# A two-layer hybrid decoder on one core: level sums and pooling from GpSimd to VectorE, the sample state's output product turned round

## The chip, the cores and the metric

The kernel runs on one core of one Trainium2 chip. The metric is the device time of one execution in microseconds (us), as a median of several runs; less is better.

## What is computed

Two layers of a decoder are run for 256 prompt tokens and 8 sample sequences of 8 tokens each, 320 tokens together (T = 320), with shared weights in float32. Cut to what matters here:

```python
def mixer(h, s_gla, buf, pos0, ...):
    proj = h @ w_in                       # q, k, v, g, a low-rank gate input, u
    gk = log_sigmoid(gk_lr @ w_gk_up + b_gk) / 16
    o, s_new = gla(q, k, v, gk, s_gla)    # S_t = diag(a_t) S_{t-1} + k_t^T v_t ; o_t = q_t S_t, a_t = exp(gk_t)
    o = rmsnorm(o, gla_norm) * silu(g)
    p, buf_new = pool_mixer(u, buf, ...)  # group i: trailing mean over (2, 4, 8, 16)[i] positions, minus the token
    return concatenate([o, p]) @ w_out, s_new, buf_new

def trunk(x, ...):
    for l in range(2):
        x = x + mixer(rmsnorm(x, norm_mix[l]), ...)
        h = rmsnorm(x, norm_ffn[l])
        x = x + (silu(h @ w_gate[l]) * (h @ w_up[l])) @ w_down[l]
    return rmsnorm(x, norm_final), states, buffers
```

There are 4 heads with keys of 128 and values of 256, a width of 2048 and a feed-forward width of 5632. The samples start from a state S of 128 x 256 for each sequence and head; the prompt starts from zero.

## The kernel before

Activations stand transposed: 128 channels on the partitions, the 320 tokens along the row, 16 such tiles for the width (`xT`). A weight is streamed in units of 128 x 1024 float32 (four tiles in the contraction, two in the output). Each unit is loaded by SP's queue (`raw`, four buffers), split by ScalarE into a rounded part and by VectorE into the rest (`hl`, three buffers, L115 and L116), and multiplied in three matmuls per tile (L151 to L153): rounded weight with rounded activation, rounded weight with the activation's rest, the weight's rest with the rounded activation. One unit is 24 matmuls, a unit of the pooling's weights 12.

`run` walks through the list of units. Before the matmuls of a unit it issues loads up to five units ahead and splits up to two units ahead; after them it gives each of the generators in `self.gens` one step. What a generator emits in its step so stands on its engine's queue behind the splits of that unit. Every engine works its queue in order. Small matmuls are put into a queue of their own by `add_small`, and `beside` places them one by one between the triples of the units' matmuls; `placed` lets a generator wait until they all stand.

What the change touches, in the order of the program:

- `first_squares`: the sum of squares of the input over the 16 tiles, for the first normalisation, and the masks' conversion. It runs beside the first units, while the input tiles (`xT`) are split into `xh` and `xl` (L118, L119).
- `level_gen`: the decays of the prompt and the samples, in eight doublings of a block length s. `P` holds the running sums of the log gates from a block's start, `X` those to a block's end, both in the tile `PX`. Each doubling takes exponentials on ScalarE (L446, L452, L456), multiplies them with q and k on VectorE (L458 to L463), adds to X on GpSimd (L466) and to P on VectorE (L468), and multiplies blocks on TensorE (L428). At s = 4 the samples' sums are complete: `e8` is their exponential, `q8` that times q.
- `ev_u` and `pool_gen`: four groups, i = 3, 2, 1, 0 with windows 16, 8, 4, 2. `ev_u` evicts the product into `EP` (prompt) and `ES` (samples) on VectorE (L595, L596) and copies the old buffer, loaded into `stg` by SP, in front of it on GpSimd (L598). `pool_gen` doubles the window on GpSimd (L614 into `AP`, L615 into `AS`), corrects the first positions (L621), copies the new buffer into `so` (L625, L626), and forms the difference `d` on VectorE, which is split into `dh` and `dl` for a pooling unit.
- `head_gen`: for each head the transposes of v, the output product, its squares and its norm, and the new states. `S` holds four sequences' states, two buffers of 128 x 4 x 256 for a head. The samples' part of the output takes, for each of 8 sequences and 2 halves of the values, one matmul with S as the weight and 8 columns of `q8` moving (L743).
- `finish`: the last norm. `rsqrt` takes a logarithm and an exponential on ScalarE and four steps on VectorE; then VectorE and GpSimd multiply the 16 tiles (L1017) and SP stores them (L1018).

The line of the old output product, and the part of `stack`, `EP` and `so` that the steps below name, are these:

```python
            for b in range(NB):
                self.add_small(224, lambda b=b: nc.tensor.matmul(
                    po[:, NP + 8 * b : NP + 8 * b + 8], S[b // 4][:, b % 4, vc],
                    st["q8"][:, h, 8 * b : 8 * b + 8], start=False, stop=(b == NB - 1)))
```

Of the kernel before, what the change touches and what calls it, by code (L numbers as in the profile page):

```python
# [66 lines left out]
class Decoder:  # L67
    def __init__(self, tc, ctx, a):
        self.tc, self.nc, self.a = tc, tc.nc, a
        nc = self.nc  # L70
        pool = lambda name, bufs, **k: ctx.enter_context(tc.tile_pool(name=name, bufs=bufs, **k))
        self.const = const = pool("const", 1)
        self.act = pool("act", 1)
        self.ffb = pool("ffb", 2)
        self.wp = pool("wp", 1)
        self.nrm = pool("nrm", 1)
        self.keep = pool("keep", 1)
        self.acc = pool("acc", 4, space=PSUM)
# [241 lines left out]
    def open_early(self):  # L320
# [7 lines left out]
        st["q8"] = self.keep.tile([P, H, 64], F32, tag="q8", name="q8")  # L328
        st["e8"] = self.keep.tile([P, H, 64], F32, tag="e8", name="e8")
# [73 lines left out]
    def level_gen(self):  # L403
# [35 lines left out]
        for li, s in enumerate((1, 2, 4, 8, 16, 32, 64, 128)):  # L439
# [26 lines left out]
            nc.gpsimd.tensor_tensor(Xv[:, :, :, 0, :], Xv[:, :, :, 0, :],  # L466
# [118 lines left out]
    def ev_u(self, ps, i):  # L585
# [12 lines left out]
        nc.gpsimd.tensor_copy(ES[:, :, :, 0:BUF], stg)  # L598
        self.gens.append(self.pool_gen(l, i, EP, ES))

    def pool_gen(self, l, i, EP, ES):
# [8 lines left out]
        while s < w:  # L610
# [3 lines left out]
            nc.gpsimd.tensor_tensor(ap[:, :, lo:], cp[:, :, lo:], cp[:, :, lo - s : np_ - s], ALU.add)  # L614
            nc.gpsimd.tensor_tensor(as_[:, :, lo:], cs[:, :, lo:], cs[:, :, lo - s : ns_ - s], ALU.add)  # L615
# [5 lines left out]
        nc.gpsimd.tensor_tensor(cp[:, :, BUF : BUF + 16], cp[:, :, BUF : BUF + 16],  # L621
# [3 lines left out]
        nc.gpsimd.tensor_copy(so[:, :, 0:NB, :], ES[:, :, :, NS:])  # L625
        nc.gpsimd.tensor_copy(so[:, :, NB, :], EP[:, :, NP:])  # L626
# [39 lines left out]

    def head_gen(self, h, vT):
# [10 lines left out]
        S = []  # L678
        for qd in range(2):
            s = late.tile([P, 4, DV], F32, tag="S", name="S", bufs=2)  # L680
            nc.sync.dma_start(out=s, in_=a["s0"][l, h, :, 4 * qd : 4 * qd + 4])
            S.append(s)
# [28 lines left out]
        o = late.tile([P, 2, T], F32, tag="o", name="o", bufs=2)  # L711
        sq = late.tile([P, 2, T], F32, tag="osq", name="osq")
# [12 lines left out]
        def state_out(qd, pss):  # L725
            for b4 in range(4):
                b = 4 * qd + b4
                nc.vector.scalar_tensor_tensor(
                    S[qd][:, b4, :], S[qd][:, b4, :], st["e8"][:, h, 8 * b + 7 : 8 * b + 8],
                    pss[b4 // 2][:, 256 * (b4 % 2) : 256 * (b4 % 2) + 256], ALU.mult, ALU.add)  # L730
            nc.sync.dma_start(out=a["s_sample"][l, h, :, 4 * qd : 4 * qd + 4], in_=S[qd])

        def out_mm(c):
# [5 lines left out]
                po[:, 128:NP], vt[:, 1, vc], self.sc[:, h, 256:384], start=False, stop=True))  # L739
            self.add_small(220, lambda: nc.tensor.matmul(  # L740
                po[:, NP:T], vs[:, vc], self.scs[:, h, :], start=True, stop=False))
            for b in range(NB):
                self.add_small(224, lambda b=b: nc.tensor.matmul(  # L743
                    po[:, NP + 8 * b : NP + 8 * b + 8], S[b // 4][:, b % 4, vc],
                    st["q8"][:, h, 8 * b : 8 * b + 8], start=False, stop=(b == NB - 1)))
            return po

        def out(c, po):
            nc.scalar.activation(o[:, c, :], po[:, :T], AF.Copy, scale=self.vec(l, V_GN, c))
            nc.scalar.activation(sq[:, c, :], po[:, :T], AF.Square)  # L750

        pos = [out_mm(0), out_mm(1)]
        yield
        yield from self.placed()
        pss = state_mm(0)
        for c in range(2):
            out(c, pos[c])
# [10 lines left out]
        pss = state_mm(1)  # L768
        yield
        yield from self.placed()  # L770
        sp = late.tile([P, 2, T], F32, tag="osq", name="sp")[:, 0, :DV]
        nc.scalar.copy(sp, pS[:, :DV])
        nc.sync.dma_start(out=a["s_prompt"][l, h], in_=sp)
        state_out(1, pss)
        ro = late.tile([P, T], F32, tag="ro", name="ro")
# [181 lines left out]
    def first_squares(self):  # L957
        nc = self.nc
        q = [self.ffb.tile([P, 8, T], F32, tag=t, name="q" + t) for t in ("ah", "al")]
        for c in range(2):  # L960
            x = self.xT[:, 4 * c : 4 * c + 4, :]
            nc.gpsimd.tensor_tensor(q[0][:, 4 * c : 4 * c + 4, :], x, x, ALU.mult)
        add = lambda a, b: nc.gpsimd.tensor_tensor(a, a, b, ALU.add)
        add(q[0][:, 0:4], q[0][:, 4:8])
        for c in range(2):
            for _ in range(2):
                yield
            v = q[1][:, 4 * c : 4 * c + 4]
            nc.scalar.activation(v, self.xT[:, 8 + 4 * c : 12 + 4 * c, :], AF.Square)
            if c == 0:  # L970
                add(q[0][:, 0:4], v)
                v = q[0]
            add(v[:, 0:2], v[:, 2:4])
            add(v[:, 0], v[:, 1])
# [27 lines left out]
    def finish(self, evacs):  # L1002
# [4 lines left out]
        nc.scalar.activation(self.warm, self.eps, AF.Ln)  # L1007
# [106 lines left out]
```

## Time and profile before

| what | value |
|---|---|
| runs | 2706.63, 2707.62, 2709.3 us; median 2707.62 |
| the profiled execution | 2707.78 us, of which the span from the first to the last instruction 2706.0 us |
| TensorE busy | 2670.5 us (99% of the span) |
| VectorE busy | 1353.6 us (50%) |
| ScalarE busy | 1067.7 us (39%) |
| GpSimd busy | 310.6 us (11%) |
| DMA | 409.06 MB, mean 151 GB/s |

The execution lies 0.16 us above the median of the runs. PE is TensorE, PEld its weight loads, DVE VectorE, ACT ScalarE, POOL GpSimd, SP the engine on whose queue all DMAs are issued. In a timeline a row has the start, the duration (of all instructions of the row, where there are several), the engine, the line, the operation, what it writes and reads, its shape and its count; in brackets the engine's idle time before it and what ended that. A matmul's own duration overlaps that of the next: what one costs is read from the distance of the starts.

### The profile page before, as it was taken

What the parts mean: (1) busy time and instruction counts of PE and PEld (TensorE: products, weight loads), DVE (VectorE), ACT (ScalarE), POOL (GpSimd) and SP (SyncE); (2) the same over time, 40 slices, a digit from 0 to 9 for tenths busy, and PEclk for the clock granted to TensorE, in tenths of its full rate; (3) what the DMA queues carried; (4) which work ended last, traced back from release to release, by engine and by line L of the source; (5) the groups of instructions that cost most, each with busy time, mean ns of one, the idle gap of its engine ahead of it and who ended that gap; (6) DMA issues with size and microseconds to landing.
All of it is one profiled execution on the core that took longest, in us unless ns stands there. A gap on an engine that the chain in (4) does not pass through costs nothing.

```text
span 2706.0 us, 44907 instructions
## 1 busy us (share of the span) xinstructions
PE 2670.5 (99%) x19046; PEld 2649.3 (98%) x19046; DVE 1353.6 (50%) x1662; ACT 1067.7 (39%) x1346; POOL 310.6 (11%) x347
## 2 busy tenths in 40 slices
PE   9999999999999999999999999999999999999997
PEld 8999999999999999999999999999999999999997
DVE  7754554544444444444658545445444444444444
ACT  5445544333333333333444554443333333333334
POOL 3521211000000000000106111100000000000002
PEclk9999999999999999999999999999999999999999
DMA  5455544444444444444443555544444444444443
GB/s 195 124 157 175 170 153 149 148 149 152 151 148 149 151 152 150 148 150 151 146 152 107 170 179 164 152 148 149 148 150 151 151 148 149 150 152 150 148 150 108
DMA packets 116217, 409.06 MB, mean 151 GB/s; under 512 B 13360, under 2 KB 16944, under 8 KB 116016
## 3 DMA queue, kind: packets, MB, share of 16 engines
q1 hardware_dynamic: 116016, 406.19, 47.9%
q8 instruction: 149, 2.44, 0.4%
q14 instruction: 52, 0.43, 0.0%
HBM read 392.98 MB, written 13.16 MB: 150 GB/s over the span
## 4 chain that ended last, share of the span: by engine, by line
PE 93%; issue 2%; DVE 2%; POOL 1%; ACT 1%; DMA 0%; DVEq 0%; SPq 0%; ACTq 0%; POOLq 0%
PE acc L151 31%; PE acc L153 30%; PE acc L152 30%; PE ps_o L743 1%; DVE hl L116 1%; POOL PX L466 0%; ACT hl L115 0%; POOL AS L615 0%; POOL AP L614 0%; PE ps_sn L719 0%; PE ps_o L736 0%; PE ps_sp L766 0%; PE ps_o L740 0%; DMA raw<-in_w_in 0%; DVE xT L1017 0%
## 5 line engine op out<-in xcount | busy, mean ns | idle before, releaser
L116 DVE TENSOR_TENSOR hl<-raw,hl 128x1024 fp32r<-128x1024 f32 (+1 forms) x729 | 923.3, 1267 | 1250.6 <-ACT hl L115 1249.6
L115 ACT CAST hl<-raw 128x1024 fp32r<-128x1024 f32 (+1 forms) x729 | 759.8, 1043 | 1291.1 <-PE acc L153 1244.4
L151 PE MATMUL acc<-xh,hl 128*128 128x320 f32 x3840 | 1212.0, 316 | 1.7 <-ACT xh L118 0.9
L153 PE MATMUL acc<-xh,hl 128*128 128x320 f32 x3840 | 1188.0, 309 | 4.2 <-DVE hl L116 4.2
L152 PE MATMUL acc<-xl,hl 128*128 128x320 f32 x3840 | 1187.4, 309 | 1.4 <-DVE xl L119 1.3
L151 PEld LDWEIGHTS acc<-xh,hl 128*128 128x128 f32 x3840 | 722.0, 188 | 6.8 <-issue 1.7
L153 PEld LDWEIGHTS acc<-xh,hl 128*128 128x128 f32 x3840 | 721.5, 188 | 5.9 <-DVE hl L116 5.6
L152 PEld LDWEIGHTS acc<-xl,hl 128*128 128x128 f32 x3840 | 722.4, 188 | 4.3 <-DVE xl L119 2.0
L153 PE MATMUL acc<-ah,hl 128*128 128x320 f32 x1408 | 435.1, 309 | 0.0
L151 PE MATMUL acc<-ah,hl 128*128 128x320 f32 x1408 | 435.1, 309 | 0.0
L152 PE MATMUL acc<-al,hl 128*128 128x320 f32 x1408 | 435.1, 309 | 0.0
L151 PEld LDWEIGHTS acc<-ah,hl 128*128 128x128 f32 x1408 | 264.3, 188 | 0.0
L152 PEld LDWEIGHTS acc<-al,hl 128*128 128x128 f32 x1408 | 264.3, 188 | 0.0
L153 PEld LDWEIGHTS acc<-ah,hl 128*128 128x128 f32 x1408 | 264.3, 188 | 0.0
L833 POOL TENSOR_TENSOR ft<-ft,r 128x320 f32<-128x320 f32 x88 | 75.4, 880 | 1641.2 <-ACT ft L832 1641.2
L275 DVE TENSOR_TENSOR xT<-xT,acc 128x320 f32<-128x320 f32 x224 | 98.4, 480 | 5.8 <-PE acc L153 5.8
L252 POOL TENSOR_TENSOR sqa<-sqa,sq 128x320 f32<-128x320 f32 x58 | 51.0, 879 | 289.6 <-ACT sq L251 287.5
L151 PE MATMUL acc<-ph,hl 128*128 128x320 f32 x256 | 80.4, 314 | 0.0
L152 PE MATMUL acc<-ol,hl 128*128 128x320 f32 x256 | 79.1, 309 | 0.0
L151 PE MATMUL acc<-oh,hl 128*128 128x320 f32 x256 | 79.1, 309 | 0.0
L153 PE MATMUL acc<-ph,hl 128*128 128x320 f32 x256 | 79.1, 309 | 0.0
L153 PE MATMUL acc<-oh,hl 128*128 128x320 f32 x256 | 79.1, 309 | 0.0
(202 smaller groups left out, 1572.8 us busy)
## 6 DMA issues: line engine op xcount, KB each, us to landing
raw<-in_w_gu SPq DMA_DIRECT2D x352, 512.0 KB, 3.6
raw<-in_w_down SPq DMA_DIRECT2D x176, 512.0 KB, 3.6
raw<-in_w_in SPq DMA_DIRECT2D x127, 512.0 KB, 4.0
raw<-in_w_out SPq DMA_DIRECT2D x64, 512.0 KB, 3.7
S<-in_s SPq DMA_DIRECT2D x16, 512.0 KB, 4.5
out_s_sample<-S SPq DMA_DIRECT2D x16, 512.0 KB, 3.3
raw<-in_w_pool SPq DMA_DIRECT2D x8, 256.0 KB, 2.9
xT<-in_xT SPq DMA_DIRECT2D x3, 640.0 KB, 7.3
```

The costliest lines, as they stand in the source:

```text
L115: nc.scalar.copy(hi, src)
L116: nc.vector.tensor_tensor(lo, src, hi.bitcast(F32), ALU.subtract)
L151: nc.tensor.matmul(ps, wh, xh, start=first, stop=False)
L152: nc.tensor.matmul(ps, wh, xl, start=False, stop=False)
L153: nc.tensor.matmul(ps, wl, xh, start=False, stop=last)
L252: nc.gpsimd.tensor_tensor(self.sq_acc, self.sq_acc, s, ALU.add)
L275: self.nc.vector.tensor_tensor(self.xT[:, m, :], self.xT[:, m, :], p, ALU.add)
L743: self.add_small(224, lambda b=b: nc.tensor.matmul(po[:, NP + 8 * b : NP + 8 * b + 8], S[b // 4][:, b % 4, vc], st["q8"][:, h, 8 * b : 8 * ...
L833: self.nc.gpsimd.tensor_tensor(t, t, self.r, ALU.mult)
```

## The change

- The sums on X go to VectorE, ahead of those on P.
- The doublings of the pooling and their correction go to VectorE; the copies into `ES` and `so` go to ScalarE.
- The first sum of squares: all four squares on ScalarE, the sums on VectorE; the masks' conversion on ScalarE.
- The samples' output product is turned round. `q8` becomes the weight, padded with zeros to 32 columns for each of 4 sequences and 2 quadruples; S moves with its 256 columns; four such matmuls write the four groups of 32 rows of one tile `ps_os`. ScalarE copies this to `qs`, and a matmul with columns of the identity turns it back and adds it to the output `ps_o`. `e8` keeps only the last position of each sequence.
- In a head the new states are written one step earlier, the first half of the next head's S is loaded one unit after the store that it follows, and the output's eviction comes one step later.
- The last norm: one table of ScalarE that has both logarithm and exponential is loaded ahead; the norm is written to PSUM (`ps_finr`), from where VectorE reads it, and ScalarE copies it for GpSimd; VectorE takes 12 tiles of the 16 where it took 11.

```diff
@@ level_gen
-            nc.gpsimd.tensor_tensor(Xv[:, :, :, 0, :], Xv[:, :, :, 0, :],
+            nc.vector.tensor_tensor(Xv[:, :, :, 0, :], Xv[:, :, :, 0, :],
                                     Pv[:, :, :, 1, s - 1 : s].to_broadcast(shape), ALU.add)
...
-                nc.scalar.activation(st["e8"], P4[:, :, NP:T], AF.Exp, scale=1.0 / GKN)
-                nc.vector.tensor_tensor(st["q8"], st["e8"], q4[:, :, NP:T], ALU.mult)
+                nc.scalar.activation(e8, P4[:, :, NP:T], AF.Exp, scale=1.0 / GKN)
+                nc.scalar.copy(st["e8"], e8[:, :, 7::8])
+                for qd in range(2):
...
+                    nc.vector.tensor_tensor(self.q8[:, :, :, qd, 8 * qd : 8 * qd + 8], part(e8),
+                                            part(q4[:, :, NP:T]), ALU.mult)
@@ ev_u, pool_gen
-        nc.gpsimd.tensor_copy(ES[:, :, :, 0:BUF], stg)
+        nc.scalar.copy(ES[:, :, :, 0:BUF], stg)
...
-            nc.gpsimd.tensor_tensor(ap[:, :, lo:], cp[:, :, lo:], cp[:, :, lo - s : np_ - s], ALU.add)
-            nc.gpsimd.tensor_tensor(as_[:, :, lo:], cs[:, :, lo:], cs[:, :, lo - s : ns_ - s], ALU.add)
+            nc.vector.tensor_tensor(ap[:, :, lo:], cp[:, :, lo:], cp[:, :, lo - s : np_ - s], ALU.add)
+            nc.vector.tensor_tensor(as_[:, :, lo:], cs[:, :, lo:], cs[:, :, lo - s : ns_ - s], ALU.add)
...
-        nc.gpsimd.tensor_copy(so[:, :, 0:NB, :], ES[:, :, :, NS:])
-        nc.gpsimd.tensor_copy(so[:, :, NB, :], EP[:, :, NP:])
+        nc.scalar.copy(so[:, :, 0:NB, :], ES[:, :, :, NS:])
+        nc.scalar.copy(so[:, :, NB, :], EP[:, :, NP:])
@@ head_gen
+        def seq4(qd):
+            for j in range(4):
+                nc.tensor.matmul(os_[32 * j : 32 * j + 32, :], self.q8[:, h, j, qd, :], S[qd][:, j, :],
+                                 start=(qd == 0), stop=(qd == 1))
...
-            for b in range(NB):
-                self.add_small(224, lambda b=b: nc.tensor.matmul(
-                    po[:, NP + 8 * b : NP + 8 * b + 8], S[b // 4][:, b % 4, vc],
-                    st["q8"][:, h, 8 * b : 8 * b + 8], start=False, stop=(b == NB - 1)))
+            self.add_small(220, lambda: nc.tensor.matmul(po[:, NP:T], qs[:, vc], rows, start=False, stop=True))
...
+        for qd in range(2):
+            self.add_small(430, lambda qd=qd: seq4(qd))
...
+        nc.scalar.copy(qs, os_)
@@ first_squares
-        for c in range(2):
-            x = self.xT[:, 4 * c : 4 * c + 4, :]
-            nc.gpsimd.tensor_tensor(q[0][:, 4 * c : 4 * c + 4, :], x, x, ALU.mult)
-        add = lambda a, b: nc.gpsimd.tensor_tensor(a, a, b, ALU.add)
+        add = lambda a, b: nc.vector.tensor_tensor(a, a, b, ALU.add)
+        acc = q[0][:, 0:4]
+        for c in range(4):
+            v = q[c // 2][:, 4 * (c % 2) : 4 * (c % 2) + 4]
+            nc.scalar.activation(v, self.xT[:, 4 * c : 4 * c + 4, :], AF.Square)
...
@@ finish
-        nc.scalar.activation(self.warm, self.eps, AF.Ln)
+        nc.scalar.preload_act_table_set("natural_log_exp_and_others")
...
-        r = self.nrm.tile([P, T], F32, tag="r", name="fin_r", bufs=2)
-        self.rsqrt(r, ps, 1.0 / D_MODEL)
-        for lo, n, eng in ((0, 1, nc.vector), (11, 2, nc.gpsimd), (1, 3, nc.vector), (4, 4, nc.vector),
-                           (13, 3, nc.gpsimd), (8, 3, nc.vector)):
+        rp = self.smt("ps_finr")[:, :T]
+        rs = self.nrm.tile([P, T], F32, tag="r", name="fin_r", bufs=2)
+        self.rsqrt(rp, ps, 1.0 / D_MODEL)
+        nc.scalar.copy(rs, rp)
+        for lo, n, eng, r in ((0, 2, nc.vector, rp), (2, 3, nc.vector, rp), (12, 2, nc.gpsimd, rs),
+                              (5, 3, nc.vector, rp), (8, 2, nc.vector, rp), (14, 2, nc.gpsimd, rs),
+                              (10, 2, nc.vector, rp)):
```

How the queues change is shown at three places. The line numbers of the changed kernel are a few higher than those of the kernel before. First VectorE in the first layer, from the second doubling's sums to the next weight split but one (`Dp`, `Ds` are the blocks of scores; `EP`, `ES`, `AP`, `AS` belong to the pooling with window 16). Before:

```order
L468 TENSOR_TENSOR PX<-PX 128x320x2
L116 TENSOR_TENSOR hl<-raw,hl 128x1024
L485 COPY_PREDICATED Dp<-masks,ps_lp 128x128
L487 COPY_PREDICATED Ds<-masks,ps_ls 64x64
L458 TENSOR_TENSOR Q<-Q,qk 128x640
L460 TENSOR_TENSOR K<-K,qk 128x1280
L116 TENSOR_TENSOR hl<-raw,hl 128x1024
```

Of the change:

```order
L468 TENSOR_TENSOR PX<-PX 128x320x2
L470 TENSOR_TENSOR PX<-PX 128x320x2
L622 TENSOR_TENSOR AP<-EP 128x2x270
L623 TENSOR_TENSOR AS<-ES 128x16x22
L119 TENSOR_TENSOR hl<-raw,hl 128x1024
L493 COPY_PREDICATED Dp<-masks,ps_lp 128x128
L495 COPY_PREDICATED Ds<-masks,ps_ls 64x64
L460 TENSOR_TENSOR Q<-Q,qk 128x640
L462 TENSOR_TENSOR K<-K,qk 128x1280
L622 TENSOR_TENSOR AP<-AP 128x2x268
L623 TENSOR_TENSOR AS<-AS 128x16x20
L119 TENSOR_TENSOR hl<-raw,hl 128x1024
```

Five instructions that stood on GpSimd's queue now stand ahead of the two weight splits. Second, ScalarE at the end of the same stage, from the last exponential of the levels (`kd`) to the eviction of the third pooling product (`ph`). Before:

```order
L520 ACTIVATE kd<-PX 128x1024
L115 CAST hl<-raw 128x512
L516 COPY sc<-ps_1740 128x4x128
L115 CAST hl<-raw 128x1024
L115 CAST hl<-raw 128x512
L115 CAST dh<-d 128x640
L115 CAST hl<-raw 128x1024
L128 ACTIVATE ph<-acc,vecs 128x320 x2
```

Of the change:

```order
L528 ACTIVATE kd<-PX 128x1024
L118 CAST hl<-raw 128x512
L606 COPY ES<-stg 128x16x15
L524 COPY sc<-ps_1742 128x4x128
L633 COPY so<-ES 128x2x120
L634 COPY so<-EP 128x2x15
L118 CAST hl<-raw 128x1024
L118 CAST hl<-raw 128x512
L118 CAST dh<-d 128x640
L118 CAST hl<-raw 128x1024
L131 ACTIVATE ph<-acc,vecs 128x320 x2
```

The copy that waits for the load of `stg` now stands on ScalarE ahead of two weight splits, and the two copies into `so` with it. Third, TensorE within a head, among the units' triples. Before, a part of the sixteen matmuls with S as the weight (each row one matmul, which runs in two passes):

```order
L743 MATMUL ps_o<-q_155,S 128x8
L151 MATMUL acc<-xh,hl 128x320
L152 MATMUL acc<-xl,hl 128x320
L153 MATMUL acc<-xh,hl 128x320
L743 MATMUL ps_o<-q_155,S 128x8
```

Of the change:

```order
L751 MATMUL ps_os<-S,q_91 32x256 x4
L154 MATMUL acc<-xh,hl 128x320
L155 MATMUL acc<-xl,hl 128x320
L156 MATMUL acc<-xh,hl 128x320
L751 MATMUL ps_os<-S,q_91 32x256 x4
```

The sixteen single matmuls of a head become two blocks of four and, in the unit behind them, two matmuls `ps_o<-ident,qs` of 64 columns.

More of the change, by code (lines that the diff above doesn't have):

```diff
@@ L94, in __init__ @@
         self.scs = self.keep.tile([64, H, 64], F32, name="scs")
+        self.q8 = self.keep.tile([P, H, 4, 2, 32], F32, name="q8")
         nc.gpsimd.memset(self.eps, EPS)
+        nc.gpsimd.memset(self.q8, 0.0)
         self.last_sq, self.mf = [], None
@@ L665, in ev_v, with load_state @@
         self.gens.append(self.head_gen(h, vT))
+    def load_state(self, l, h, qd):
+        s = self.late.tile([P, 4, DV], F32, tag="S", name="S", bufs=2)
+        self.nc.sync.dma_start(out=s, in_=self.a["s0"][l, h, :, 4 * qd : 4 * qd + 4])
+        self.st.setdefault("S", {}).setdefault(h, []).append(s)
     def head_gen(self, h, vT):
@@ L677, in head_gen @@
             yield
[L678 to L682, printed above, removed]
+        if h == 0:
+            self.load_state(l, 0, 0)
+        self.load_state(l, h, 1)
+        S = st["S"].pop(h)
         p1, p2, p3 = self.smt("ps_vt"), self.smt("ps_vs"), self.smt("ps_vq")
@@ L739, in out_mm, with out_mm2 @@
                 po[:, 128:NP], vt[:, 1, vc], self.sc[:, h, 256:384], start=False, stop=True))
+            return po
+        def out_mm2(c, po):
+            vc = slice(128 * c, 128 * c + 128)
             self.add_small(220, lambda: nc.tensor.matmul(
                 po[:, NP:T], vs[:, vc], self.scs[:, h, :], start=True, stop=False))
-            for b in range(NB):
-                self.add_small(224, lambda b=b: nc.tensor.matmul(
-                    po[:, NP + 8 * b : NP + 8 * b + 8], S[b // 4][:, b % 4, vc],
-                    st["q8"][:, h, 8 * b : 8 * b + 8], start=False, stop=(b == NB - 1)))
-            return po
+            self.add_small(220, lambda: nc.tensor.matmul(po[:, NP:T], qs[:, vc], rows, start=False, stop=True))
         def out(c, po):
             nc.scalar.activation(o[:, c, :], po[:, :T], AF.Copy, scale=self.vec(l, V_GN, c))
-            nc.scalar.activation(sq[:, c, :], po[:, :T], AF.Square)
+            nc.scalar.activation(sq[c], po[:, :T], AF.Square)
         pos = [out_mm(0), out_mm(1)]
+        for qd in range(2):
+            self.add_small(430, lambda qd=qd: seq4(qd))
         yield
         yield from self.placed()
+        qs = late.tile([P, DV], F32, tag="qs", name="qs")
+        nc.scalar.copy(qs, os_)
         pss = state_mm(0)
         for c in range(2):
-            out(c, pos[c])
-        nc.gpsimd.tensor_tensor(sq[:, 0, :], sq[:, 0, :], sq[:, 1, :], ALU.add)
+            out_mm2(c, pos[c])
         yield
         yield from self.placed()
-        state_out(0, pss)
+        o = late.tile([P, 2, T], F32, tag="o", name="o", bufs=2)
+        sq = [self.nrm.tile([P, T], F32, tag="sq", name="osq", bufs=2) for _ in range(2)]
+        for c in range(2):
+            out(c, pos[c])
+        nc.gpsimd.tensor_tensor(sq[0], sq[0], sq[1], ALU.add)
+        state_out(0, pss)
+        pss = state_mm(1)
+        yield
+        yield from self.placed()
+        if h + 1 < H:
+            self.load_state(l, h + 1, 0)
+        state_out(1, pss)
         pr = self.smt("ps_or")
-        self.add_small(540, lambda: nc.tensor.matmul(pr[:, :T], self.ones, sq[:, 0, :], start=True, stop=True))
+        self.add_small(540, lambda: nc.tensor.matmul(pr[:, :T], self.ones, sq[0], start=True, stop=True))
         pS = self.smt("ps_sp")
@@ L767, in head_gen @@
                 pS[:, :DV], st["kdt"][:, t, 128 * h : 128 * h + 128], vt[:, t, :], start=(t == 0), stop=(t == 1)))
-        pss = state_mm(1)
         yield
         yield from self.placed()
-        sp = late.tile([P, 2, T], F32, tag="osq", name="sp")[:, 0, :DV]
+        sp = late.tile([P, DV], F32, tag="qs", name="sp")
         nc.scalar.copy(sp, pS[:, :DV])
         nc.sync.dma_start(out=a["s_prompt"][l, h], in_=sp)
-        state_out(1, pss)
-        ro = late.tile([P, T], F32, tag="ro", name="ro")
+        ro = self.nrm.tile([P, T], F32, tag="sqa", name="ro")
         self.rsqrt(ro, pr[:, :T], 1.0 / DV)
```

37 lines of the change are left out of this document (17 added, 20 removed).

## The prediction

> **What bounds the kernel now.** I read the page first, then the busy times by stretch, then TensorE's timeline where its matmuls stand further apart than elsewhere, and the queues of VectorE, ScalarE and GpSimd at those places. The page:
>
> ```profile
> span 2706.0 us, 44907 instructions
> PE 2670.5 (99%) x19046; PEld 2649.3 (98%) x19046; DVE 1353.6 (50%) x1662; ACT 1067.7 (39%) x1346; POOL 310.6 (11%) x347
> ```
>
> TensorE is the bound. A busy share of 99% says little, though, since a matmul's duration overlaps the next. The stretches (us; busy time and count of PE, PEld, DVE, ACT, POOL; granted clock) say more:
>
> ```profile
> 0.00:40.00 40.00, 33.83 (x196) 32.32 (x197) 32.29 (x30) 23.61 (x33) 21.35 (x17) 0.96 0.68 231
> 120.00:160.00 40.00, 38.77 (x347) 36.96 (x346) 35.12 (x49) 21.21 (x35) 22.55 (x24) 0.96 0.42 127
> 560.00:600.00 40.00, 40.00 (x275) 40.00 (x274) 18.77 (x22) 14.38 (x18) 1.72 (x2) 1.00 0.50 155
> ```
>
> In the feed-forward part 275 matmuls fill 40 us, 0.147 us from start to start. The units hold 17,376 such matmuls (as many as the groups that write acc count), 2549 us in all, which the change leaves alone. The other 157 us are the start, the two stages of levels and pooling (93 to 167 us and the same in the second layer), the small matmuls of the heads, and the end. Every part of the change falls into one of these four.
>
> **1. The start.** GpSimd squares and adds while VectorE splits inputs and weights:
>
> ```profile
> 6.34 1.01 DVE L119 SCALAR_TENSOR_TENSOR xl<-xT,vecs,xh 128x320 fp32r<-128x320 f32 x2
> 11.03 3.34 DVE L116 TENSOR_TENSOR hl<-raw,hl 128x1024 fp32r<-128x1024 f32 x1
> 14.29 4.65 DVE L119 SCALAR_TENSOR_TENSOR xl<-xT,vecs,xh 128x320 fp32r<-128x320 f32 x4
> 21.13 6.58 DVE L119 SCALAR_TENSOR_TENSOR xl<-xT,vecs,xh 128x320 fp32r<-128x320 f32 x4
> 48.76 1.23 DVE L116 TENSOR_TENSOR hl<-raw,hl 128x1024 fp32r<-128x1024 f32 x1 [1.06 <-ACT hl L115]
> ```
>
> ```profile
> 10.95 2.34 POOL L962 TENSOR_TENSOR qah<-xT 128x1280 f32<-128x1280 f32 x1 [1.31 <-DMA xT<-in_xT]
> ```
>
> ```profile
> 10.70 0.64 PE L152 MATMUL acc<-xl,hl 128*128 128x320 f32 x1 [1.30 <-DVE xl L119]
> 20.13 0.42 PE L153 MATMUL acc<-xh,hl 128*128 128x320 f32 x1 [1.34 <-DVE hl L116]
> 28.91 0.41 PE L153 MATMUL acc<-xh,hl 128*128 128x320 f32 x1 [1.48 <-DVE hl L116]
> ```
>
> A weight split takes 1.23 us when GpSimd is idle and 3.34 us when its sums run; four input splits take 4.65 and 6.58 us instead of 2.0 (two in 1.01). VectorE is so late that TensorE waits three times, 1.30 + 1.34 + 1.48 = 4.1 us. The change takes these sums off GpSimd. VectorE gets five adds: three of 1280 elements (1.5 us each, worked out from 1.23 for 1024), one of 640 and one of 320: 5.8 us. The three rows above alone give back 2.1 + 2.6 + 4.5 = 9.2 us. ScalarE gets two more squares and the masks, 1.3 us each by its own rate, in the idle time before its casts. The splits then end 2 to 4 us before TensorE asks. Of 4.1 us I take 4.0; the ends are 2.0 (the added work falls just ahead of the splits) and 5.0 (the shorter waits beside them go too). GpSimd's setup instruction ahead of its first sum moves to the first head. Here nothing of it shows in the rows, and it was hidden by at most the 6.5 us up to 7.3; there it runs while ScalarE still squares. 0 us.
>
> **2. Levels and pooling.** VectorE's groups from 93.4 to 167 us (busy, mean in ns | idle before them):
>
> ```profile
> L116 DVE TENSOR_TENSOR hl<-raw,hl 128x1024 fp32r<-128x1024 f32 x14 | 21.0, 1502 | 0.5 <-ACT hl L115 0.2
> L468 DVE TENSOR_TENSOR PX<-PX 128x512 f32<-128x512 f32 x5 | 6.0, 1191 | 3.2 <-POOL PX L466 3.2
> L468 DVE TENSOR_TENSOR PX<-PX 128x640 f32<-128x640 f32 x2 | 3.4, 1692 | 1.8 <-POOL PX L466 1.8
> ```
>
> and what such sums take beside an idle GpSimd, with the end of the stage on all engines:
>
> ```profile
> 86.32 0.82 DVE L468 TENSOR_TENSOR PX<-PX 128x640 f32<-128x640 f32 x1
> 137.41 0.69 DVE L468 TENSOR_TENSOR PX<-PX 128x512 f32<-128x512 f32 x1
> ...
> 154.60 1.22 DVE L116 TENSOR_TENSOR hl<-raw,hl 128x1024 fp32r<-128x1024 f32 x1
> 156.94 1.05 ACT L115 CAST hl<-raw 128x1024 fp32r<-128x1024 f32 x1
> 159.84 0.40 POOL L598 COPY ES<-stg 128x240 f32<-128x240 f32 x1 [7.01 <-DMA stg<-in_bufT]
> 162.27 0.85 DVE L632 SCALAR_TENSOR_TENSOR d<-AP,EP 128x512 f32<-128x512 f32 x1 [1.50 <-POOL AP L621]
> 163.58 0.73 ACT L115 CAST dh<-d 128x640 fp32r<-128x640 f32 x1 [3.55 <-DVE d L634]
> 165.29 1.22 DVE L116 TENSOR_TENSOR hl<-raw,hl 128x1024 fp32r<-128x1024 f32 x1
> 166.44 1.00 DVE L133 SCALAR_TENSOR_TENSOR pl<-acc,vecs,ph 128x320 fp32r<-128x320 f32 x2
> 167.04 0.41 PE L151 MATMUL acc<-dh,hl 128*128 128x320 f32 x1 [1.51 <-DVE pl L133]
> ```
>
> VectorE gets, in each layer, seven sums on X in this stretch (2 x 0.82 + 5 x 0.69 = 5.1 us), ten doublings of some 520 elements (0.70 each, 7.0), ten of 128 to 352 (some 0.35 each by the same slope, 3.5), four corrections (0.2 each, 0.8): 16.4, less 0.08 for each of 31, since starts follow that much closer than durations: 13.9 us. It gets back 14 x 0.28 + 5 x 0.50 + 2 x 0.87 = 8.1 us of stretch in the three groups, 5.0 us of waiting for GpSimd's sums, and some 4 us in the smaller groups. So VectorE's stage ends a few us earlier at most, and until the last pooling unit it carries TensorE's waits along.
>
> Then comes a chain that VectorE doesn't set. The load of stg is issued when the split at 154.60 has ended; the copy starts at 159.84, 4.0 us after that end. Now this copy stands on ScalarE ahead of the cast that ran at 156.94. From the split's end: 4.0, the copies into ES, sc and so with the cast 2.3, VectorE's two splits and d 2.6, the cast dh 0.8, dl, a split and the first pl 2.4: 12.1 us, where the rows have 166.98 - 155.82 = 11.2. The split itself I put 1.6 us earlier: 17.1 us back less 13.9 added is 3.2, and half of that I leave to the same wait at the second-last group. So TensorE's wait at 167.04 ends 0.7 us earlier, in each layer: 1.4 us. The ends: 5 us a layer gained (VectorE's account in full, no wait of ScalarE on the path), or 2 us lost (every one of the four waits costs a cast 0.5 us more). I take the value near the chain's end, because the last wait decides what stays.
>
> **3. The heads.** TensorE around the removed matmuls, and its one block that writes 32 columns at a time:
>
> ```profile
> 190.41 0.31 PE L153 MATMUL acc<-xh,hl 128*128 128x320 f32 x1
> 190.56 0.28 PE L743 MATMUL ps_o<-q,S 128*128 128x8 f32 x2
> ...
> 191.07 0.31 PE L153 MATMUL acc<-xh,hl 128*128 128x320 f32 x1
> ```
>
> ```profile
> 47.34 0.31 PE L153 MATMUL acc<-xh,hl 128*128 128x320 f32 x1
> 47.58 2.36 PE L375 MATMUL ps_gk<-xT,gkw 128*32 128x320 f32 x32
> 49.87 0.42 PE L151 MATMUL acc<-xh,hl 128*128 128x320 f32 x1
> ```
>
> From L153 to L153 are 0.66 us with one L743 between, 0.44 without (3 x 0.147): 0.22 us for each, 3.55 us for the 16 of a head. No wait stands ahead of TensorE there, so what goes is gained in full. L375 is the same form as the new block: 16 matmuls, four after another into four groups of 32 rows, 32 passes of 320 columns in 2.29 us, where one after another they would need at least 32 x 0.147 = 4.7 even at the rate of the rounded format. Four share the array, then: 2.13 us are eight rounds of 0.267 us, and entering and leaving add some 0.35 with the slower start behind it. A new block is two rounds of 256 columns (2 x 0.213 = 0.43) and the same 0.35: 0.78. Per head 2 x 0.78, and two matmuls with the identity like L743 (one weight load a pass) 2 x 0.22: 2.0 us. Gain 1.55 a head, 12.4 us for eight. Ends: 14 and more if entering costs half (17), 10 if the second block pays more. ScalarE's copy of 128 x 256 a head lies in its idle time, as does the later eviction. The next head's S is loaded earlier, past fewer of SP's weight loads: 0.
>
> **4. The end.**
>
> ```profile
> 2686.89 0.31 PE L153 MATMUL acc<-ah,hl 128*128 128x320 f32 x1
> 2689.19 0.53 ACT L139 ACTIVATE rs_t<-ps_fin,small 128x320 f32<-128x320 f32 x1 [0.30 <-PE ps_fin L1011]
> 2689.74 1.28 ACT L140 ACT_TABLE_LOAD   x1
> 2691.03 0.47 ACT L140 ACTIVATE rs_y<-rs_t 128x320 f32<-128x320 f32 x1
> 2693.11 7.38 DVE L1017 TENSOR_TENSOR xT<-xT,fin_r 128x320 f32<-128x320 f32 x4
> 2693.15 4.92 POOL L1017 TENSOR_TENSOR xT<-xT,fin_r 128x640 f32<-128x640 f32 x2 [10.04 <-DVE fin_r L144]
> ```
>
> ```profile
> 2702.00:2703.00 1.00, 0.00 (x0) 0.00 (x0) 0.00 (x0) 0.00 (x0) 0.00 (x0) 0.50 1.03 403
> ```
>
> The table load between logarithm and exponential goes: 1.3 us. The Trainium skill, in "ScalarE: Activation LUTs", section "What ACT_TABLE_LOAD costs", adds a drain of about 1.38 us to each load. Here the exponential starts 1.31 us after the logarithm's end, load included, so the trace shows no such drain; by the page this term would be 2.7 and the time 1.4 us less.
>
> VectorE's multiplications take 7.38 us for 11 tiles, against 3.9 without GpSimd beside it (0.35 a tile). With the norm in PSUM they should run at that rate: the pl of the row at 166.44, which read PSUM too, took 0.5 us each while GpSimd copied. They start 0.5 us later, behind ScalarE's copy of the norm. Twelve tiles then take 4.3 us. The stores become the limit: 16 tiles are 2.6 MB, 6.5 us at 403 GB/s, and the second can't start before its three tiles are there. From the norm's end: 0.5 for the copy, 0.8 for the first two tiles, 0.9 to the transfer, 6.5, a gap of 0.3, and 1.5 from the last packet to the end: 10.5, where it was 12.9 (2706.0 - 2693.1). 2.4 and 1.3 give 3.7 us; ends 2.0 (VectorE still stretched by half) and 4.5.
>
> **The sum.** 4.0 + 1.4 + 12.4 + 3.7 = 21.5 us off the profiled 2707.78 gives 2686.3; off the median of 2707.62, 2686.1. I predict 2686.
>
> **Rivals.** *The stages of levels gain in full.* For it: 5.0 us of waits for GpSimd and the stretched splits go, and TensorE waits on VectorE alone there. Against it: the chain over stg. At 5 us a layer instead of 0.7 the time is 2677.5. *The four column groups run one after another.* Eight passes of 0.213 and 0.35 make a block 2.05 us instead of 0.78; over 16 blocks 20.3 us, and the time is 2706.3, no change. L375's 2.29 us speak against it. *ScalarE held by stg, slower.* In each layer ScalarE stops four times until stg lands; casts, exponentials and all of VectorE behind it stop as well. A load takes about 4 us from the split that frees SP's queue. If each wait fell on the path in full, eight times 4 us, the stages would lose 32 instead of gaining 1.4: 2719.5. It outweighs the other parts (20.1 us) from 2.5 us a wait and is plainly slower from 3.2. Against it: at the first two groups the load lands before ScalarE comes to it. *The change to the start and the end gives half*: 2690.
>
> **How the numbers follow.** A measurement of this kernel tells about 0.2% (5.4 us) from no change. My case has 0.58 (2680 to 2691 with its own bounds), the full gain in the stages 0.20, half at the start and end 0.12 (up to 2695), serial groups 0.06, ScalarE held 0.04. The range goes from 2677, the full gain, to 2695, and leaves out the last two cases and the tails. Faster 0.91, same 0.06, slower 0.03.
>
> **What would show it.** Start: L119 at 0.5 us each throughout and no wait for VectorE at the units from 18 us on. Stages: L468 at 0.69, a wait of the copy into ES for DMA on ScalarE, and a wait of the last pooling unit for pl that is still there. Heads: eight passes into ps_os within 0.8 us between two triples. End: one table load less, multiplications of 960 elements near 1.15 us, stores at 400 GB/s without a gap of over 0.5 us. Wrong it would be if passes into ps_os stood 0.2 us apart, or if TensorE waited some us at each of the four groups.

## The result, and the profile after

The changed kernel takes 2686.28 us (2685.63 to 2687.35, four runs) against 2707.74 us: ratio 0.9921, interval 0.9904 to 0.9938, or 21.5 us less. The forecast was 2686. The sum agrees; its terms do so less well, so that the time came out within 0.3 us of the forecast is partly luck. The page of the changed kernel (2685.63 us in the profiled execution), and the busy times in the stretches shown of before:

```profile
span 2683.7 us, 44716 instructions
PE 2653.9 (99%) x18950; PEld 2621.3 (98%) x18950; DVE 1347.9 (50%) x1734; ACT 1078.9 (40%) x1382; POOL 199.2 (7%) x250
```

```profile
0.00:40.00 40.00, 36.42 (x228) 34.66 (x229) 28.87 (x44) 28.92 (x39) 2.75 (x8) 1.00 0.79 267
120.00:160.00 40.00, 37.67 (x344) 35.52 (x332) 33.17 (x63) 20.40 (x39) 5.75 (x12) 1.00 0.47 144
560.00:600.00 40.00, 40.00 (x275) 40.00 (x274) 17.18 (x19) 14.04 (x17) 3.42 (x4) 1.00 0.47 146
```

In the first 40 us TensorE runs 228 matmuls where it ran 196, in the feed-forward part 275 as before; from 120 to 160 us 344, where it ran 347. That last pair says little, since the whole stage now stands some 5 us earlier and the window holds other work. To place every microsecond, the start of each of the 17,376 matmuls into acc was compared with that of the same matmul before. What the changed kernel gains up to a mark less what it gained up to the mark ahead is a stretch's own gain (from the two profiled executions, whose spans differ by 22.3 us):

| stretch (us of the span) | forecast | measured |
|---|---|---|
| start, up to the 216th matmul | -4.0 | -5.33 |
| levels and pooling, first and second layer | -0.7, -0.7 | -0.38, -0.10 |
| the heads, first and second layer | -6.2, -6.2 | -6.47, -6.47 |
| from the last matmul's start to the end | -3.7 | -3.53 |
| all | -21.5 | -22.27 |

The start gave 1.3 us more than forecast and the levels 0.9 less; the sum hides it.

The start, on VectorE (the splits' lines are now L119 for weights, L122 for inputs):

```profile
7.04 1.00 DVE L122 SCALAR_TENSOR_TENSOR xl<-xT,vecs,xh 128x320 fp32r<-128x320 f32 x2
14.68 1.23 DVE L119 TENSOR_TENSOR hl<-raw,hl 128x1024 fp32r<-128x1024 f32 x1 [0.33 <-ACT hl L118]
19.37 1.93 DVE L122 SCALAR_TENSOR_TENSOR xl<-xT,vecs,xh 128x320 fp32r<-128x320 f32 x4
```

A weight split takes 1.23 us throughout, four input splits 1.93 where they took 4.65 and 6.58. The stages, first as VectorE's groups from 88 to 161 us, then at the places where ScalarE, VectorE and TensorE stand still:

```profile
L119 DVE TENSOR_TENSOR hl<-raw,hl 128x1024 fp32r<-128x1024 f32 x14 | 17.1, 1219 | 1.9 <-ACT hl L118 1.6
L470 DVE TENSOR_TENSOR PX<-PX 128x512 f32<-128x512 f32 x5 | 3.5, 692 | 0.2
L468 DVE TENSOR_TENSOR PX<-PX 128x512 f32<-128x512 f32 x5 | 3.4, 679 | 0.0
```

```profile
129.39 0.42 SPq L600 DMA_DIRECT2D stg<-in_bufT  x1
132.87 0.40 ACT L606 COPY ES<-stg 128x240 f32<-128x240 f32 x1 [4.62 <-DMA stg<-in_bufT]
133.83 0.69 DVE L460 TENSOR_TENSOR Q<-Q,qk 128x512 f32<-128x512 f32 x1 [1.78 <-ACT Q L448]
152.80 0.40 ACT L606 COPY ES<-stg 128x240 f32<-128x240 f32 x1 [3.16 <-DMA stg<-in_bufT]
```

```profile
111.69 0.39 PE L154 MATMUL acc<-dh,hl 128*128 128x320 f32 x1 [0.93 <-DVE ES L604]
115.73 0.52 PE L573 MATMUL ps_kq<-ident,kq 128*128 128x128 f32 x3 [1.60 <-DVE Ds L495]
135.18 1.15 PE L513 MATMUL ps<-Q,K 128*64 128x64 f32 x16 [0.90 <-DVE K L465]
156.35 0.42 PE L156 MATMUL acc<-xh,hl 128*128 128x320 f32 x1 [0.70 <-DVE hl L119]
161.32 0.41 PE L154 MATMUL acc<-dh,hl 128*128 128x320 f32 x1 [1.47 <-DVE pl L136]
```

The stretch of the splits is gone (1219 ns for 1502) and so are VectorE's waits for GpSimd's sums. In their place ScalarE stands 4.62 and 3.16 us behind the copy that waits for stg, and VectorE 1.78 us behind ScalarE. Over the whole span the copy waits for stg six times of eight (who waits, for whom, us in total, times, longest):

```profile
ACT ES L606 <- DMA stg<-in_bufT: 19.4, 6, 4.9
```
TensorE's first wait here was this one in the kernel before:

```profile
119.23 0.39 PE L151 MATMUL acc<-dh,hl 128*128 128x320 f32 x1 [3.14 <-DVE ES L596]
...
120.15 0.47 PE L153 MATMUL acc<-dh,hl 128*128 128x320 f32 x1
120.42 0.47 PE L151 MATMUL acc<-dh,hl 128*128 128x320 f32 x1
```

It is now 0.93 us, and this is the early gain. Behind the old wait the granted clock was 0.50 from 120 to 122 us as well (the last two rows stand 0.27 us apart instead of 0.147), so the twelve matmuls of this unit took 2.52 us from the first start to the last; they now take 1.69, at a clock of 1.00. The wait for Ds behind them grew (0.33 to 1.60 us of idle time), one for K is new, one for hl at 156.35 us is too, and the last one, for pl, stayed (1.51 before). The heads, and the end:

```profile
185.91 0.64 PE L751 MATMUL ps_os<-S,q 128*32 128x256 f32 x8
186.47 0.41 PE L154 MATMUL acc<-xh,hl 128*128 128x320 f32 x1
190.56 0.33 PE L767 MATMUL ps_o<-ident,qs 128*128 128x64 f32 x2
```

```profile
2670.45 0.53 ACT L142 ACTIVATE rs_t<-ps_fin,small 128x320 f32<-128x320 f32 x1 [0.30 <-PE ps_fin L1040]
2671.01 0.47 ACT L143 ACTIVATE rs_y<-rs_t 128x320 f32<-128x320 f32 x1
2673.10 0.42 ACT L1044 COPY fin_r<-ps_finr 128x320 f32<-128x320 f32 x1 [1.62 <-DVE ps_finr L147]
2673.55 4.41 DVE L1049 TENSOR_TENSOR xT<-xT,ps_finr 128x640 f32<-128x640 f32 x5 [0.49 <-ACT fin_r L1044]
2673.60 3.05 POOL L1049 TENSOR_TENSOR xT<-xT,fin_r 128x640 f32<-128x640 f32 x2 [9.21 <-ACT fin_r L1044]
```

The eight passes into ps_os (two for each of the four matmuls) are over 0.56 us behind the first one's start, and add 0.76 us (mean of all 16 blocks: from the last matmul of the triple ahead to the last of the triple behind, less three times 0.147). The exponential follows the logarithm without a table load, and VectorE's 12 tiles take 4.41 us beside GpSimd.

### The profile page after: what moved, and what is told of

It reads as the page before. It is cut to its first block, busy times and chain, and to the rows that moved or that the text cites. A ratio compares the mean times of both kernels' runs of the same rounds, so it can differ in the third digit from the quotient of the medians.

```text
span 2683.7 us, 44716 instructions
## 1 busy us (share of the span) xinstructions
PE 2653.9 (99%) x18950; PEld 2621.3 (98%) x18950; DVE 1347.9 (50%) x1734; ACT 1078.9 (40%) x1382; POOL 199.2 (7%) x250
## 4 chain that ended last, share of the span: by engine, by line
PE 93%; DVE 4%; ACT 1%; DMA 1%; issue 1%; SPq 0%; DVEq 0%; ACTq 0%
PE acc L154 30%; PE acc L156 30%; PE acc L155 30%; DVE hl L119 1%; DMA stg<-in_bufT 1%; ACT hl L118 0%; DVE AP L622 0%; PE ps_os L751 0%; DMA xT<-in_xT 0%; DVE PX L468 0%; DVE K L462 0%; PE ps_sn L729 0%; PE ps_sp L801 0%; PE ps_o L757 0%; DVE PX L470 0%
## 5 line engine op out<-in xcount | busy, mean ns | idle before, releaser
L119 DVE TENSOR_TENSOR hl<-raw,hl 128x1024 fp32r<-128x1024 f32 (+1 forms) x729 | 911.4, 1251 | 1228.2 <-ACT hl L118 1227.5
L155 PE MATMUL acc<-pl,hl 128*128 128x320 f32 x256 | 79.1, 309 | 0.0
```

The source lines that it names most:

```text
L119: nc.vector.tensor_tensor(lo, src, hi.bitcast(F32), ALU.subtract)
L155: nc.tensor.matmul(ps, wh, xl, start=False, stop=False)
```

## The experiments

Times are medians; behind each stands the difference to the kernel before on the same chip (2708.40, 2707.51 and 2707.81 us in the three sets). The eleven other kernels whose start is that of the changed kernel won between 3.8 and 6.3 us there. In four of these eleven traces (all back on GpSimd, only the pooling back, stg early, and the order for Ds) TensorE's granted clock fell to 0.50 between 8 and 16 us, and these four won 3.8 to 4.6; the other seven won 5.4 to 6.3. So the kernels of the levels are compared by the sum of their two stages in the traces, as in the table above: -0.48 us for the changed kernel. Three kernels further down, whose levels are those of the changed kernel (the blocks of three and one, the constant sums, the norm in SBUF), come to -1.25, -0.23 and -0.57: less than about 1 us between two kernels' stages tells nothing.

### Levels: who does the work, and when stg comes

**All of it back on GpSimd.** Edit: `nc.vector` to `nc.gpsimd` for the sums on X, the doublings and the corrections, `nc.scalar.copy` to `nc.gpsimd.tensor_copy` for the copies into ES and so.

> The changed kernel (2686.3 us), with the sums on X, the doublings, the corrections and the small copies of the pooling back on GpSimd; start, heads and end stay changed. By the prediction's own term (0.7 us a layer) it takes 1.4 us more, 2687.7. By the changed kernel's trace, where TensorE leaves the two stages no earlier than before (0.03 us earlier in the first layer, 0.25 later in the second), it takes 2686.1, a difference that cannot be told from none. If the full-gain rival were right (5 us a layer), 2696.

2687.07 us (-21.3); its stages +1.27. The whole move is worth 1.75 us in the changed kernel, near the 1.4 that I had put on it, and far from the 10 of the full gain. The stages with the old placement are 1.27 us slower than before. What stays changed in them is a copy into e8 on ScalarE and a second multiplication into q8 on VectorE, at s = 4; whether that is the reason was not tested.

**Each part by itself.** Edits: only the sums back, or only the pooling with its copies back.

> The changed kernel with only the sums on X back on GpSimd; the doublings stay on VectorE and the small copies on ScalarE. Theory A (VectorE's account: what it is given equals what it is spared, each part for itself nearly nothing): within 1 us of 2686.3. Theory B (the move of the sums gains some 2 to 3 us a layer, and ScalarE's waits for stg, 4.62 and 3.16 us in the first layer, give them back): VectorE waits for GpSimd's sums again and ScalarE for stg as well, 2 to 3 us more a layer, 2690 to 2692.

> The changed kernel with the pooling (doublings, corrections, copies into ES and so) back on GpSimd; the sums on X stay on VectorE. ScalarE has no wait for stg then. Theory A (VectorE's account): within 1 us of 2686.3. Theory B (the sums gain, ScalarE's waits for stg give it back): the gain shows, 1 to 3 us less a layer, 2680 to 2684.

2685.19 us (-23.2), stages -0.98; 2685.91 us (-22.5), stages -1.43. Both look like theory A: each half is within 1 us of the whole, and so cannot be told from it. Theory B's price for the sums was wrong. In both stg is loaded as late as before.

**stg one group earlier.** Edit: two tiles for stg instead of one; the first load is issued with the last q (not shown), each further one behind the copy of the group ahead.

```diff
+    def load_stg(self, i):
+        self.stg = self.early.tile([P, 2, NB, BUF], F32, tag="stg", name="stg", bufs=2)
+        self.nc.sync.dma_start(out=self.stg, in_=self.a["bufT"][self.st["l"], :, 2 * i : 2 * i + 2])
...
         nc.scalar.copy(ES[:, :, :, 0:BUF], stg)
+        if i:
+            self.load_stg(i - 1)
```

> The changed kernel, with the old buffer loaded one group earlier into one of two tiles (the first with the last q), so that ScalarE's copy into ES never waits for DMA; nothing else is moved. Theory B (ScalarE's wait for stg gives the gain back): ScalarE's idle 4.62 and 3.16 us before that copy go, VectorE's idle 1.78 us (for Q) and 1.9 us (for ES and the next cast) behind them too, and TensorE's waits of 1.20 and 0.65 us in the middle and about half of the 3.1 us at the end: 3 us a layer, 2680.3. Theory A (VectorE's account): the waits turn into others, 2685.3 to 2687.3.

2678.61 us (-29.8), stages -7.58: 7.1 us won by the load alone. TensorE's waits in this kernel's first stage:

```profile
112.43 0.39 PE L154 MATMUL acc<-dh,hl 128*128 128x320 f32 x1 [0.92 <-DVE ES L608]
116.48 0.63 PE L574 MATMUL ps_kq<-ident,kq 128*128 128x128 f32 x4 [1.62 <-DVE Ds L496]
129.79 0.41 PE L156 MATMUL acc<-xh,hl 128*128 128x320 f32 x1 [0.16 <-DVE hl L119]
158.78 0.42 PE L154 MATMUL acc<-dh,hl 128*128 128x320 f32 x1 [1.30 <-DVE pl L136]
```

The waits that were at 135.18 and 156.35 us are gone, the others stand. So the late load took back the gain, as theory B has it. Is it the load, or that ScalarE waits for it? Two runs ask that.

> The kernel with the sums and the whole pooling back on GpSimd (2687.1 us), and stg loaded one group earlier. With stg early and the work on VectorE and ScalarE it was 2678.6. Theory B (the late stg hides what the move to VectorE is worth): with GpSimd doing the work, stg is waited for only at the last group (7 us of GpSimd's idle time end with it, and VectorE's d waits 1.5 us behind); an early load gives at most 1.5 us a layer, 2684 to 2687, and the move is worth 5 to 8 us once stg is early. Theory C (the late load costs the same whoever does the work, and the move is worth nothing either way): 2679 to 2680.

> The changed kernel with only the copy from stg into ES back on GpSimd, stg loaded as late as before. Theory B1 (what costs is that ScalarE stands still behind that copy, with exponentials and casts that have nothing to do with stg): the landing (132.8 and 152.8 us in the first layer) is hardly later than VectorE needs ES, so most of the gain of the early load comes, 2680 to 2682. Theory B2 (what costs is that ES is late, whoever copies): little is gained, 2685 to 2687.

With GpSimd doing all the work the early load gives 4.4 us: 2682.51 us (-25.0), stages -3.14. That is more than the 3 us that theory B allowed and less than the 7.1 that theory C needs. With only the copy into ES back on GpSimd and stg as late as before, 2682.18 us (-25.3), stages -4.25: 3.8 of the 7.1 us come from ScalarE's queue not standing still, somewhat less than expected. The rest stays behind the late landing; the copies into so now wait on ScalarE, and VectorE waits for ES:

```profile
ACT so L633 <- POOL ES L606: 4.4, 2, 3.3
DVE AS L623 <- POOL ES L606: 0.9, 1, 0.9
```

(From this kernel's waits of 93 to 167 us: who waited, for whom, us in total, times, longest.)

**Each part by itself, with stg early.** The edits of the two halves and that of the load together.

> The changed kernel with stg early (2678.6 us), only the sums on X back on GpSimd. With stg early and both parts on GpSimd it was 2682.5, so the two parts together are worth 4.4 us in the traces' two stages. If the doublings and copies carry that: 2678 to 2679. If the sums carry it: 2682 to 2683. If they share it: 2680.5.

> The changed kernel with stg early (2678.6 us), only the pooling (doublings, corrections, small copies) back on GpSimd, the sums on X on VectorE. If the doublings and copies carry the 4.4 us: 2682 to 2683. If the sums carry them: 2678 to 2679. If they share it: 2680.5.

2675.64 us (-32.2), stages -10.31, further than any of the three guesses; 2684.14 us (-23.7), stages -2.48: the doublings and copies carry it all. All eight cells (sum of both stages against before, us):

| | stg late | stg early |
|---|---|---|
| all on GpSimd | +1.27 | -3.14 |
| sums on X on GpSimd, pooling moved | -0.98 | **-10.31** |
| sums on X moved, pooling on GpSimd | -1.43 | -2.48 |
| both moved (the change) | -0.48 | -7.58 |

With stg early, moving the pooling gains 7.2 us (5.1 with the sums moved too), and moving the sums on X loses 2.7 (with the pooling on GpSimd 0.7, too little to be told from none). With stg late all four rows lie within 2.7 us. The clock has a part in this: in both cells with stg early and the pooling on GpSimd TensorE waits 2.4 to 2.9 us for ES, and its granted clock is 0.50 behind that wait in both layers; in the two cells with the pooling moved the wait is 0.9 to 1.6 us and the clock stays at 1.00. How much of the 7.2 and 5.1 us that is was not separated. The best kernel of the study is the changed one with stg early and the sums on X left on GpSimd. No wait for pl shows any more; what TensorE waits for in its first stage:

```profile
111.64 0.39 PE L154 MATMUL acc<-dh,hl 128*128 128x320 f32 x1 [1.64 <-DVE ES L608]
115.17 0.63 PE L574 MATMUL ps_kq<-ident,kq 128*128 128x128 f32 x4 [1.10 <-DVE Ds L496]
```

**The wait for Ds, and the order at the end.** Edit to the kernel with stg early and both moved: `pend()` moved from behind the sums to ahead of them, and in `finish` `nc.scalar.copy(rs, rp)` behind the first multiplication.

> The changed kernel with stg early (2678.6 us), the copies of the scores into Dp and Ds one step earlier, ahead of the sums and the doublings, and at the end VectorE's first two tiles ahead of ScalarE's copy of the norm. The wait of TensorE of 1.89 us between the two ps_kq, which ends with VectorE's copy into Ds, goes to under 0.7 us in each layer, of which part comes back at the next wait that VectorE ends (0.47 us 13 us later): 1.2 to 1.9 us a layer. At the end VectorE starts 0.45 us earlier, and the stores with it. Sum: 2675.4, from 2674.5 to 2677. If VectorE's account alone decided, the earlier copies would only move the wait and it would stay at 2678.

2679.31 us (-28.2), stages -8.21: 0.6 us for the two layers, not 2.4 to 3.8, and no more than such sums differ by themselves. The wait for Ds is gone. In this kernel's timeline two others stand at that place and 13 us behind it:

```profile
116.49 0.41 PE L156 MATMUL acc<-xh,hl 128*128 128x320 f32 x1 [0.91 <-DVE hl L119]
129.78 0.41 PE L156 MATMUL acc<-xh,hl 128*128 128x320 f32 x1 [0.60 <-DVE hl L119]
```

The second was 0.16 us. Here VectorE's account does decide: one queue that is late stays late, whichever of its items TensorE meets first. At the end nothing was won either. VectorE's first two tiles are 0.45 us earlier, but the third waits for ScalarE's read of the same PSUM tile, where the first had waited (timeline of this kernel):

```profile
2667.41 3.68 DVE L1054 TENSOR_TENSOR xT<-xT,ps_finr 128x960 f32<-128x960 f32 x4 [0.49 <-ACT fin_r L1057]
```

### Heads: do the four column groups run together?

Edit: `seq4(qd)` becomes `seq4(qd, js)`, placed once with `js = (0, 1, 2)` and once with `js = (3,)`.

> The changed kernel with each block of four matmuls into ps_os cut into one of three column groups and one of the fourth, each between two triples. Theory parallel (a block takes two passes of one group and a fixed cost of entering and leaving, however many groups are in it): the block of three costs 0.77 us as that of four did, the single one 0.7 to 0.8 on top, for 16 blocks 11 to 13 us, 2698.5. Theory serial (the cost grows with the matmuls): three quarters and a quarter of 0.77 and at most 0.35 for the second entry, 0 to 5.6 us, 2686 to 2692.

2697.85 us (-9.7); the span is 11.8 us longer than the changed kernel's. In the timeline a block of three groups and a block of one take the same time:

```profile
185.62 0.63 PE L751 MATMUL ps_os<-S,q 128*32 128x256 f32 x6
186.18 0.41 PE L154 MATMUL acc<-xh,hl 128*128 128x320 f32 x1
...
186.81 0.62 PE L751 MATMUL ps_os<-S,q 128*32 128x256 f32 x2
187.36 0.41 PE L154 MATMUL acc<-xh,hl 128*128 128x320 f32 x1
```

Over the 16 blocks each, three add 0.75 us, one 0.74, and four added 0.76. The groups run together, and the cost is that of one group's two passes and of entering and leaving.

### Start: what stretches VectorE

Edit, behind the first memsets of `first_squares`: `for _ in range(8): nc.gpsimd.tensor_tensor(self.sc, self.sc, self.sc, ALU.add)`.

> The changed kernel, and GpSimd adds a constant tile of zeros to itself eight times (128 x 1536 each) from 3.3 us on; nothing waits for these sums and the result is the same. Theory lock (VectorE's splits of two inputs in SBUF are stretched while GpSimd's two-input sums run, and that is what the move at the start takes away): the weight splits go from 1.23 to 2 us and more, four input splits from 1.93 to over 4, TensorE waits for VectorE again up to 35 us, 4 to 9 us more, 2690 to 2695. Rival (the start is won by the order of the queues and by the shorter chain of sums): no change, 2686.3.

2700.11 us (-7.7), 14.4 us more in the start, beyond the 4 to 9 expected. From the timeline, and one row of the busy times by stretch (granted clock behind GpSimd's count):

```profile
3.33 24.65 POOL L1002 TENSOR_TENSOR sc<-sc 128x1536 f32<-128x1536 f32 x8
6.64 5.99 DVE L122 SCALAR_TENSOR_TENSOR xl<-xT,vecs,xh 128x320 fp32r<-128x320 f32 x2
18.79 0.64 PE L155 MATMUL acc<-xl,hl 128*128 128x320 f32 x1 [4.94 <-DVE xl L122]
```

```profile
12.00:14.00 2.00, 1.17 (x3) 0.77 (x3) 2.00 (x2) 2.00 (x4) 1.92 (x2) 0.50 0.87 355
```

No instruction waits for these sums, and still an input split takes 3.0 us instead of 0.5. That is the length of one GpSimd sum (24.65 / 8 = 3.08): VectorE gets one instruction done for each of GpSimd's. The Trainium skill, "SBUF — State Buffer", section "Who interferes with whom", says that a VectorE instruction with two inputs in SBUF contends with a GpSimd instruction that reads SBUF, and that such contention is an exclusive lock; this trace agrees, with 3.0 us for a split beside sums of 3.08. TensorE's granted clock, 0.50 in the last row and for some 16 us, is the part of the loss that I had not counted.

### End: the norm in PSUM

Edit: the norm goes to an SBUF tile that VectorE and GpSimd both read, and the copy is left out.

> The changed kernel with the last norm in SBUF, read there by VectorE and GpSimd alike, without ScalarE's copy. Theory lock: VectorE starts 0.45 us earlier, but its multiplications of 960 elements go from 1.15 to about 2 us as long as GpSimd's two run (some 4 us), the third and fifth stores come late, a gap of 1 to 1.5 us between the stores comes back: the end, now 15.5 us from the last unit's matmul to the end of the span, becomes 16.3 to 16.8. Rival (the stores at 390 to 400 GB/s set the end whatever the engines do): 15.1, 0.45 less. The time itself moves by at most 1.3 us.

2686.38 us (-21.4); the end takes 16.75 us instead of 15.55, inside the 16.3 to 16.8 of theory lock. The multiplications in the timeline, and the busy times of one microsecond (the last two columns are the DMA engines' share and GB/s):

```profile
2672.47 7.10 DVE L1047 TENSOR_TENSOR xT<-xT,fin_r 128x640 f32<-128x640 f32 x5
2672.59 4.51 POOL L1047 TENSOR_TENSOR xT<-xT,fin_r 128x640 f32<-128x640 f32 x2 [8.81 <-DVE fin_r L147]
```

```profile
2675.00:2676.00 1.00, 0.00 (x0) 0.00 (x0) 1.00 (x2) 0.00 (x0) 1.00 (x1) 0.50 0.03 8
```

7.10 us for the 12 tiles instead of 4.41, and a microsecond in which almost nothing is stored. In the whole time these 1.2 us do not show, since the start of this execution was 0.5 us shorter and the runs spread over more.

## Right and wrong, step by step

**Start: the mechanism right, the term too small** (4.0 forecast; 5.3 here, 5.4 in the mean over the eleven others). What I mis-sized is the waits' price: I counted idle time and left out that TensorE goes slower behind them. The kernel before had this in its busy times by stretch (the column behind POOL's count is the granted clock):

```profile
10.00:12.00 2.00, 1.30 (x5) 1.30 (x6) 2.00 (x4) 1.44 (x4) 1.05 (x1) 0.67 1.02 419
12.00:14.00 2.00, 2.00 (x9) 2.00 (x9) 2.00 (x1) 1.77 (x3) 1.92 (x2) 0.50 1.03 421
```

From 11.13 to 14.06 us its 11 matmuls stand 0.267 us apart instead of 0.147, 1.3 us lost. In the trace of the changed kernel the clock is 1.00 in every such stretch. That sums on GpSimd stretch the splits, and that TensorE then waits, is shown by the run with the constant sums (which are longer and denser than the old ones, so their 14.4 us are no measure of the old loss). The halved clock is not theirs alone: four of the other eleven traces have it too, with GpSimd idle there. Those four won 4.4 us in the mean, near the 4.0 of the forecast; the seven others and the changed kernel, at full clock, 5.8. So the size of this term hangs on the clock, and which of the two an execution gets was not traced.

**Levels: the new wait right, its place incomplete, the term too large** (1.4 forecast, 0.48 measured; 0.23 to 1.25 in the three other kernels with the same levels). Three of a layer's four copies wait for stg; I had said that the first two find it there, which holds for the second alone. I carried the last wait in full and left 1.6 us to the one before it; on TensorE that one came out as 0.90 us of idle time at 135.18 us. The starts of the matmuls give the first layer's account. Not in the sum at all were 2.22 us won at the wait of the first pooling unit (3.14 to 0.93) and 0.82 by its matmuls at full clock, of which the wait for Ds took 0.69 back; another 0.82 came from two waits for splits that are gone (0.20 and 0.70 us). Of these 3.17 us, 1.46 went again between 135 and 137 us, 0.87 at 156.35 us and 0.46 in smaller steps; 0.38 were left. That the waits for stg are what took the gain back, and not VectorE's work alone, is shown by the early load, which wins 7.1 us and leaves neither the wait at 135.18 nor that at 156.35 us.

**The rival of the full gain** fell for this kernel, but not as a possibility: with stg early and the sums on X on GpSimd the stages gain 10.3 us, the 5 a layer that it priced. **The rival of the held ScalarE** named a real mechanism at too high a price: 19.4 us of waiting in both layers cost at most the 7.1 us that the early load gave back, not 32.

**VectorE's account** (16.4 us of work for 17.1 us back) held in that the halves alone change little while stg is late. It hid that with stg early the two halves have opposite signs: the pooling's move gains, that of the sums on X loses. For the sums the reason may be that VectorE pays 0.68 us for each of its own (L468) and less for standing beside GpSimd's; for the doublings, that d waits for the last of a row of dependent steps, and that the clock halves behind the long wait for ES. None of these reasons was tested by itself.

**Heads: right** (12.4 forecast, 12.9 measured): a block 0.76 us for 0.78, a turned-back matmul 0.22 as forecast, an old pair of passes 0.22.

**End: right** (3.7 and 3.53). The table load was worth 1.28 us: 1.84 us from logarithm to exponential before, 0.56 now. VectorE's tiles took 4.41 us (4.3 forecast), its start waited for ScalarE's copy, and from the norm's end to the span's end are 10.6 us (10.5). The stores moved 302 and 310 GB/s from 2675 to 2677 us and 387 to 406 from there to 2682, without a gap. The drain that the Trainium skill, "ScalarE: Activation LUTs", section "What ACT_TABLE_LOAD costs", adds to a load does not show: 1.28 us went with the load, not 2.7.

## What to carry to other kernels

Before work is moved to another engine, look at what its queue will stand behind: one small copy that waits for a load turned ScalarE's spare time into a wait of everyone, and loading that operand earlier was worth more (7.1 us) than the whole move (1.75 us). Two moves that look like one should be priced and tried one by one, after the load that covers both is out of the way; here, with that load early, one gained 5 to 7 us and the other lost up to 2.7. And a wait of TensorE is not priced by its idle time alone, since the clock may be halved behind it.

## What was not expected of the hardware

TensorE's granted clock fell to 0.50 for some 3 us behind two waits of 0.9 and 1.3 us in the first 11 us, and for 16 us in the run with the constant sums. No length of wait was found that decides it: behind a wait of 2.4 us in the levels the clock fell with only the pooling back and stg early, and stayed at 1.00 with the pooling back and stg late. VectorE beside GpSimd did not share at some ratio, but finished about one instruction for each of GpSimd's: the longer GpSimd's instruction (3.08 us), the worse for VectorE's short ones (0.5 us). A block of one column group costs as much as one of four (0.74 and 0.76 us).
